# ScalarE and VectorE instruction order in a mixture-of-experts stage: scheduler's order or source order

## Chip, cores and metric

One core of a Trainium2 chip runs one program. The metric is device time in microseconds. Three runs of the kernel before gave 1894.52, 1895.95 and 1896.77; their median is 1895.95 us.

## What is computed

A hybrid layer, a retention layer and a Fourier layer, each with its feed-forward part, run over 256 tokens of width 1024 in float32. The change is in the last feed-forward part, a mixture of eight experts of which each token uses two:

```python
def swiglu(t, w_gate, w_up, w_down):
    return (jax.nn.silu(t @ w_gate) * (t @ w_up)) @ w_down

def moe_swiglu(h, w_router, w_gate, w_up, w_down):
    ...
    logits = (t @ w_router).astype(jnp.float32)
    top_val, top_idx = lax.top_k(logits, TOP_K)
    top_w = jax.nn.softmax(top_val, axis=-1)
    gates = jnp.sum(jax.nn.one_hot(top_idx, N_EXPERTS, dtype=jnp.float32) * top_w[..., None], axis=1)
    ...
    for e in range(N_EXPERTS):
        out = out + gates[:, e:e + 1] * swiglu(t, w_gate[e], w_up[e], w_down[e])
```

`w_gate` and `w_up` of an expert are 1024 x 3584, `w_down` is 3584 x 1024.

## The kernel before

**Weights.** All weights come as 1 MB units of 128 x 2048 float32, in the order in which TensorE uses them. SyncE issues one load a unit (line 113) into one of 13 buffers: six of `rawp`, four and two of the pools that `more_room` opens, and one in the space of `xT`. A unit is used as two *halves* of 128 x 1024. A half is split in two operands before TensorE takes it: ScalarE copies it to the short float type (line 139, tile `ringh` or `extrah`), and VectorE subtracts the copy from the original to get the rest (line 140, `ringl` or `extral`). There are six places for split halves: four in `ring`, two in `extra`, used in turn. A place is free when TensorE has done with the half in it; a raw buffer is free when VectorE has split its second half, and the next load waits for that.

**Keeping ahead.** `half` hands TensorE the oldest split half and first splits one more, so that in the source five halves stand split ahead of the one in use.

**One expert.** An expert is 84 halves in seven *strips*. In `experts`, `gate_strip` takes four halves (matmuls of lines 1154 to 1156) and ScalarE turns the sum into `sg` with Silu (line 1189). `up_strip` takes four more, and VectorE makes `h` of that sum and `sg` (line 1196). `turn` transposes `h` on TensorE (line 1206 or 1208); ScalarE and VectorE split the result into `hx` (lines 1212 and 1213). `down` takes four halves against `hx`. The `turn` of one strip lies in the middle of the next strip's gate, and its `down` behind the next strip's `up`; from the third strip on the cycle is: two gate halves, turn, two gate halves, four up halves, four down halves. At the expert's end `result` splits the two sums (lines 1245 and 1246), and `combine` adds them to `acc` during the next expert (lines 1265 to 1268).

**Packed experts.** In `up_strip`, `turn` and `down` a branch on TensorE (line 1162) takes one of two programs by the expert's number of tokens: with at most 64 (*packed*) a half costs four matmuls, otherwise six. Gate halves always cost six. In the trace, turns of line 1206 are packed ones: experts 0, 2, 3 and 4. Experts 1, 5, 6 and 7 are not.

**Hooks.** `nexth` counts halves and calls hooks at some of them: `gather` of the next expert's tokens (lines 1105 to 1124, at halves 77 to 83), `combine` (at 4 and 8) and, in expert 0, `weights_of_tokens` (at 4): about twenty small VectorE instructions, one Exp on ScalarE and one small matmul.

**What sets the order.** TensorE and SyncE run in source order in the whole kernel (`manual_schedule`). ScalarE and VectorE have no such rule in the experts: a scheduler places their instructions when the program is built. Each engine then executes its list from front to back, so that an instruction that waits holds those behind it.

Of the kernel before, what the change touches and what calls it, by code (L numbers as in the profile page):

```python
# [63 lines left out]
def kernel(  # L64
# [64 lines left out]
    def split(scales=None, between=None):  # L129


        if not raw or (half_[1] == H_F2 and scales is None):
            return
        wh, wl = place(half_[1])
        half_[1] += 1
        r = raw[0][0][:, half_[0] * HU:(half_[0] + 1) * HU]
        if scales is None:
            for o in (slice(0, HQ), slice(HQ, HU)) if half_[1] == 1 else (slice(0, HU),):
                nc.scalar.activation(out=wh[:, o], in_=r[:, o], func=AF.Copy)  # L139
                nc.vector.tensor_tensor(out=wl[:, o], in0=r[:, o], in1=wh[:, o].bitcast(F32), op=ALU.subtract)  # L140
                if between is not None and o.start == 0:
                    between()
        else:
            for t in range(2):
                o = slice(t * 512, t * 512 + 512)
                nc.scalar.activation(out=wh[:, o], in_=r[:, o], func=AF.Copy, scale=scales[:, t:t + 1])
                nc.vector.scalar_tensor_tensor(out=wl[:, o], in0=r[:, o], scalar=scales[:, t:t + 1],
                                               in1=wh[:, o].bitcast(F32), op0=ALU.mult, op1=ALU.subtract)
        wq.append((wh, wl))
        if half_[0]:  # L150
            fetch(raw.pop(0)[1])
        half_[0] ^= 1
# [39 lines left out]
    def bank(tag="mm", shape=(P, 2, S)):  # L192
        return psp.tile(list(shape), F32, tag=tag, name=tag, bufs={"mm": 4, "sd": 2, "dn": 2}[tag])
# [10 lines left out]
    def unitT(xh, xl):  # L204

        ps = bank()
        for cb in range(2):
            u = half()
            for k in range(KD):
                mm3T(ps[:, cb], u, k, xh[:, k], xl[:, k], k == 0, k == KD - 1)  # L210
        return ps

    def unit_late(xh, xl, late=2):

        ps = [bank("mm", (P, S)) for _ in range(2)]
        us = []
        for cb in range(2):
            us.append(half(ahead=not cb))
            for k in range(KD - late):
                mm3T(ps[cb], us[cb], k, xh[:, k], xl[:, k], k == 0, False)  # L220
        for cb in range(2):
            for k in range(KD - late, KD):
                mm3T(ps[cb], us[cb], k, xh[:, k], xl[:, k], False, k == KD - 1)
        split()
        return ps
# [159 lines left out]
    with pa:  # L385
# [264 lines left out]
        for i in range(8):  # L650
            ps = unitT(xh, xl)
            c, h = divmod(i, 2)
# [28 lines left out]
        for c in range(4, KD, 2):  # L681
            gg = []
            for _ in range(2):
                g = B.tile([P, 4, S], F32, tag="gate2", name="gate2")
                for h in range(2):
                    ps = unitT(xh, xl)
# [63 lines left out]
    with ExitStack() as pr:  # L750
# [120 lines left out]
        for c in range(KD):  # L871
            ps = bank("mm", (P, S))
# [23 lines left out]
    with ExitStack() as pn:  # L896
# [65 lines left out]
        def to_tok(src, c, tag):  # L962

            ps = bank(tag, (P, 2, S))
            for t in range(2):
                for b in range(2):
                    nc.tensor.transpose(ps[:, t, b * P:(b + 1) * P], src[c + b][:, t * P:(t + 1) * P], ident)
            return ps, slice(c * P, c * P + S)
# [18 lines left out]
        for cc in range(4):  # L987
            ps = unit_late(zh, zl) if cc == 0 else unitT(zh, zl)
# [34 lines left out]
        for c in range(0, KD, 2):  # L1023
            ps, o = to_tok(xT_, c, "mm")
            nc.scalar.activation(out=acc[:, :, o], in_=ps, func=AF.Copy)

        ps = bank("sd", (P, 3, E))
# [19 lines left out]
    def weights_of_tokens():  # L1047

        sel = [Q.tile([P, 2, E], F32, name=f"sel{i}") for i in range(2)]
        w12 = [Q.tile([P, 2], F32, name=f"w{i}") for i in range(2)]  # L1050
        tmp = Q.tile([P, 2, E], F32, name="tmp8")
        for i in range(2):
            nc.vector.tensor_scalar(out=sel[i], in0=cnt, scalar1=float(i), scalar2=None, op0=ALU.is_equal)
            nc.vector.tensor_tensor(out=tmp, in0=sel[i], in1=L, op=ALU.mult)
            nc.vector.tensor_reduce(out=w12[i], in_=tmp, axis=AX.X, op=ALU.add)
        nc.vector.tensor_tensor(out=w12[1], in0=w12[1], in1=w12[0], op=ALU.subtract)
        nc.vector.tensor_tensor(out=w12[1], in0=w12[1], in1=rcol, op=ALU.mult)
        nc.scalar.activation(out=w12[1], in_=w12[1], func=AF.Exp)
        nc.vector.tensor_scalar(out=w12[0], in0=w12[1], scalar1=1.0, scalar2=None, op0=ALU.add)
        nc.vector.reciprocal(out=w12[0], in_=w12[0])  # L1060
        nc.vector.tensor_tensor(out=w12[1], in0=w12[1], in1=w12[0], op=ALU.mult)
        for i in range(2):
            nc.vector.tensor_tensor(out=sel[i], in0=sel[i], in1=w12[i].unsqueeze(2).to_broadcast([P, 2, E]), op=ALU.mult)
        nc.vector.tensor_tensor(out=gts, in0=sel[0], in1=sel[1], op=ALU.add)
        ovf = Q.tile([P, 2], F32, name="ovf")
        nc.vector.tensor_scalar(out=tmp, in0=pos, scalar1=float(P), scalar2=None, op0=ALU.is_gt)
        nc.vector.tensor_reduce(out=ovf, in_=tmp, axis=AX.X, op=ALU.add)
        ps = bank("sd", (P, 2))
        mm(ps, ones, ovf, start=True, stop=True)
        nc.vector.tensor_copy(out=ovi, in_=ps)  # L1070
# [8 lines left out]
    with ExitStack() as pe:  # L1079
# [48 lines left out]
        def experts(ex, rs, half_fn, hooks=None, n_of=None):  # L1128
# [10 lines left out]
            def nexth(**kw):  # L1139
                if hooks and n[0] in hooks:  # L1140
                    hooks[n[0]]()
                n[0] += 1
                return half_fn(**kw)

            def hi_lo(x, items, packed):

                for out_, k, wh, wl, first, last in items:
                    xk = x[:, k].rearrange("p a b -> p (a b)")
                    if packed:
                        e = xk[:, HS:HS + P]  # L1150
                        mm(out_, e, wh, start=first, stop=False)
                    else:
                        e = xk[:, 0:P]
                        mm(out_, e, wh, start=first, stop=False)  # L1154
                        mm(out_, xk[:, P:2 * P], wh, start=False, stop=False)  # L1155
                    mm(out_, e, wl, start=False, stop=last)  # L1156
# [10 lines left out]
            def strip_items(ps, h, w):  # L1167
                return [(ps, 2 * h + kk, w[0][:, kk * 512:(kk + 1) * 512], w[1][:, kk * 512:(kk + 1) * 512],
                         h + kk == 0, h == 3 and kk == 1) for kk in range(2)]

            def strip(mid=None):
                ps = bank("mm", (P, 512))
                for h in range(4):
                    if h == 2 and mid is not None:
                        mid()
                    hi_lo(ex, strip_items(ps, h, nexth()), False)
                return ps

            def pair(f):
# [80 lines left out]
        def combine(res, sot, gcol, hfs=range(2)):  # L1260
            for hf in hfs:
                yh, yl = res[hf]
                for t in range(2):
                    ps = bank("sd", (P, 512))
                    mm(ps, sot[:, t], yh, start=True, stop=False)
                    mm(ps, sot[:, t], yl, start=False, stop=True)
                    o = slice(hf * 512, hf * 512 + 512)
                    nc.vector.scalar_tensor_tensor(out=acc[:, t, o], in0=ps, scalar=gcol(t), in1=acc[:, t, o],
                                                   op0=ALU.mult, op1=ALU.add)

        def gath(e):
            return gather(lambda t: pos[:, t, e:e + 1], lambda t: posu[:, t, e:e + 1])
# [4 lines left out]
        nxt = gath(0)  # L1277
# [3 lines left out]
        while len(wq) < WB + WX - 1:  # L1281
            split()
        last = None
        for e in range(E):
            ex, sot, rs, _ = nxt
            if last:
                hooks = {4: lambda a=last: combine(*a, (0,)), 8: lambda a=last: combine(*a, (1,))}
            else:
                hooks = {1: nxt[3][4], 4: weights_of_tokens}
            if e + 1 < E:  # L1290
                nxt = gath(e + 1)
                hooks.update(zip((77, 79, 80, 82, 83), nxt[3]))
            last = (experts(ex, rs, half, hooks, lambda: n_of(e)), sot, lambda t, e=e: gts[:, t, e:e + 1])
            if e == 0:
                n_over = [nc.values_load(ovi[0:1, t:t + 1], min_val=0, max_val=2 * S) for t in range(2)]
        v4 = Q.tile([P, 2, 2], F32, name="v4")
        v = Q.tile([P, 2], F32, name="fv")
        r = Q.tile([P, 2], F32, name="fr")
# [21 lines left out]
        with tc.tile_pool(name="O", bufs=1) as O:  # L1320
# [5 lines left out]
            with tc.If(n_over[0] + n_over[1] > 0):  # L1326

                nc.vector.tensor_copy(out=ecur, in_=io8)
                with tc.For_i(0, E, 1) as ev:
# [21 lines left out]
                    oex, osot, ors, steps = gather(lambda t: epos[:, t:t + 1], lambda t: epos[:, t:t + 1])  # L1351
# [179 lines left out]
```

## Time and profile before

| | |
|---|---|
| median of three runs | 1895.95 us |
| the profiled execution, its own time | 1900.18 us |
| its span in the profile | 1898.4 us |
| TensorE, matmuls | 1827.2 us, 96% of the span |
| VectorE | 1474.8 us, 78% |
| ScalarE | 1198.2 us, 63% |
| first and last Silu of the experts begin at | 912.4 and 1864.1 us |

Time lines count from the start of the span. The experts fill the second half of it. A busy share is an average over stages that have different limits: for a change in the experts it must be read there, expert by expert and strip by strip.

### The profile page before, as it was taken

What the parts mean: (1) busy time and instruction counts of PE and PEld (TensorE: products, weight loads), DVE (VectorE), ACT (ScalarE), POOL (GpSimd) and SP (SyncE); (2) the same over time, 40 slices, a digit from 0 to 9 for tenths busy, and PEclk for the clock granted to TensorE, in tenths of its full rate; (3) what the DMA queues carried; (4) which work ended last, traced back from release to release, by engine and by line L of the source; (5) the groups of instructions that cost most, each with busy time, mean ns of one, the idle gap of its engine ahead of it and who ended that gap; (6) DMA issues with size and microseconds to landing.
All of it is one profiled execution on the core that took longest, in us unless ns stands there. A gap on an engine that the chain in (4) does not pass through costs nothing. (4 is left out here: it accounts for less than half of the span.)

```text
span 1898.4 us, 28758 instructions
## 1 busy us (share of the span) xinstructions
PE 1827.2 (96%) x10890; PEld 1576.7 (83%) x10890; DVE 1474.8 (78%) x1855; ACT 1198.2 (63%) x1484; POOL 158.6 (8%) x154
## 2 busy tenths in 40 slices
PE   8999999999999999999999999999999999999996
PEld 7999999998888999998777886666676778788785
DVE  5666676657776666556899889899899988988887
ACT  5765454445444444445887777777777877767774
POOL 2302122211100122101000000000000000000000
PEclk9999999999999999999999999999999999999998
DMA  7344555555344654454799998999999999899880
GB/s 308 136 154 174 182 178 183 195 178 195 139 160 155 239 218 178 180 199 158 295 421 370 353 364 329 373 359 362 378 350 369 362 352 368 336 354 363 322 334 35
DMA packets 71156, 505.77 MB, mean 266 GB/s; under 512 B 7888, under 2 KB 8016, under 8 KB 10320
## 3 DMA queue, kind: packets, MB, share of 16 engines
q1 hardware_dynamic: 70992, 503.53, 70.5%
q8 instruction: 110, 1.80, 0.4%
q14 instruction: 54, 0.44, 0.1%
HBM read 502.45 MB, written 1.05 MB: 265 GB/s over the span
## 5 line engine op out<-in xcount | busy, mean ns | idle before, releaser
L140 DVE TENSOR_TENSOR ringl<-raw,ringh 128x1024 fp32r<-128x1024 f32 (+1 forms) x694 | 828.7, 1228 | 191.9 <-ACT ringh L139 186.6
L139 ACT ACTIVATE ringh<-raw 128x1024 fp32r<-128x1024 f32 (+1 forms) x694 | 703.4, 1050 | 309.0 <-PE mm L201 192.1
L200 PE MATMUL mm<-xh,ringh 128*128 128x256 f32 x1248 | 357.4, 286 | 6.4 <-ACT xh L354 6.4
L202 PE MATMUL mm<-xh,ringl 128*128 128x256 f32 x1248 | 354.7, 284 | 1.5 <-DVE ringl L140 1.5
L201 PE MATMUL mm<-xl,ringh 128*128 128x256 f32 x1248 | 355.1, 285 | 1.0 <-DVE xl L355 0.7
L140 DVE TENSOR_TENSOR extral<-raw,extrah 128x1024 fp32r<-128x1024 f32 x206 | 244.4, 1221 | 66.3 <-ACT extrah L139 66.3
L200 PEld LDWEIGHTS mm<-xh,ringh 128*128 128x128 f32 x1248 | 238.0, 191 | 7.8 <-ACT xh L354 6.4
L201 PEld LDWEIGHTS mm<-xl,ringh 128*128 128x128 f32 x1248 | 237.8, 191 | 2.3 <-DVE xl L355 2.1
L202 PEld LDWEIGHTS mm<-xh,ringl 128*128 128x128 f32 x1248 | 237.7, 190 | 1.9 <-DVE ringl L140 1.9
L139 ACT ACTIVATE extrah<-raw 128x1024 fp32r<-128x1024 f32 x206 | 207.6, 1050 | 10.2 <-PE mm L1155 8.2
L1156 PE MATMUL mm<-ringl,ex 128*128 128x512 f32 x480 | 191.0, 398 | 0.0
L1156 PE MATMUL mm<-extral,ex 128*128 128x512 f32 x416 | 168.0, 404 | 17.3 <-DVE extral L140 17.0
L1156 PE MATMUL dn<-ringl,hx 128*128 128x512 f32 x416 | 170.5, 410 | 0.0
L1154 PE MATMUL mm<-ringh,ex 128*128 128x512 f32 x352 | 144.4, 410 | 0.0
L1155 PE MATMUL mm<-ringh,ex 128*128 128x512 f32 x352 | 139.8, 397 | 0.2 <-DVE ex L1115 0.2
L1154 PE MATMUL mm<-extrah,ex 128*128 128x512 f32 x320 | 125.5, 392 | 0.0
L1155 PE MATMUL mm<-extrah,ex 128*128 128x512 f32 x320 | 125.4, 392 | 0.0
L1156 PEld LDWEIGHTS mm<-extral,ex 128*128 128x128 f32 x416 | 78.0, 187 | 53.4 <-DVE extral L140 38.2
L1156 PEld LDWEIGHTS mm<-ringl,ex 128*128 128x128 f32 x480 | 90.6, 189 | 24.1 <-DVE ringl L140 2.3
L1156 PEld LDWEIGHTS dn<-ringl,hx 128*128 128x128 f32 x416 | 78.2, 188 | 38.6 <-DVE ringl L140 23.1
L202 PE MATMUL mm<-hh,ringl 128*128 128x256 f32 x352 | 99.6, 283 | 0.0
L200 PE MATMUL mm<-hh,ringh 128*128 128x256 f32 x352 | 99.6, 283 | 0.0
(420 smaller groups left out, 3158.8 us busy)
## 6 DMA issues: line engine op xcount, KB each, us to landing
raw<-in_ws_dram SPq DMA_DIRECT2D x448, 1024.0 KB, 6.7
xT<-in_ws_dram SPq DMA_DIRECT2D x25, 1024.0 KB, 7.5
raw<-in_ws_dram SPq DMA_DIRECT2D x3, 512.0 KB, 7.8
xT<-in_xT_dram SPq DMA_DIRECT2D x4, 256.0 KB, 4.7
xT<-in_xT_dram SPq DMA_DIRECT2D x1, 1024.0 KB, 8.2
out_dram<-acc SPq DMA_DIRECT2D x4, 256.0 KB, 2.1
cstA<-in_cst_dram SPq DMA_DIRECT2D x1, 576.0 KB, 9.5
raw<-in_ws_dram SPq DMA_DIRECT2D x2, 256.0 KB, 4.2
```

Source lines behind the costliest of these rows:

```text
L139: nc.scalar.activation(out=wh[:, o], in_=r[:, o], func=AF.Copy)
L140: nc.vector.tensor_tensor(out=wl[:, o], in0=r[:, o], in1=wh[:, o].bitcast(F32), op=ALU.subtract)
L200: mm(ps, wh[:, c], xh, start=start, stop=False)
L201: mm(ps, wh[:, c], xl, start=False, stop=False)
L202: mm(ps, wl[:, c], xh, start=False, stop=stop)
L1154: mm(out_, e, wh, start=first, stop=False)
L1155: mm(out_, xk[:, P:2 * P], wh, start=False, stop=False)
L1156: mm(out_, e, wl, start=False, stop=last)
```

## The change

ScalarE and VectorE get source order from the start of the experts' loop to its end (`manual_schedule`, closed behind the loop). For that, three things in the source move: `strip` now asks for its third half before it calls the turn, `weights_of_tokens` becomes a generator whose four steps run at halves 4, 5, 6 and 7, and the load of the two overflow counts (`values_load` of `ovi`, on every engine) now stands where the source has it.

```diff
@@ -1055,7 +1055,9 @@
             nc.vector.tensor_reduce(out=w12[i], in_=tmp, axis=AX.X, op=ALU.add)
         nc.vector.tensor_tensor(out=w12[1], in0=w12[1], in1=w12[0], op=ALU.subtract)
         nc.vector.tensor_tensor(out=w12[1], in0=w12[1], in1=rcol, op=ALU.mult)
+        yield
         nc.scalar.activation(out=w12[1], in_=w12[1], func=AF.Exp)
+        yield
         nc.vector.tensor_scalar(out=w12[0], in0=w12[1], scalar1=1.0, scalar2=None, op0=ALU.add)
...
@@ -1065,6 +1067,7 @@
         nc.vector.tensor_reduce(out=ovf, in_=tmp, axis=AX.X, op=ALU.add)
+        yield
         ps = bank("sd", (P, 2))
...
@@ -1171,9 +1174,10 @@
                 for h in range(4):
+                    w = nexth()
                     if h == 2 and mid is not None:
                         mid()
-                    hi_lo(ex, strip_items(ps, h, nexth()), False)
+                    hi_lo(ex, strip_items(ps, h, w), False)
                 return ps
...
@@ -1281,18 +1285,22 @@
         last = None
+        order = ExitStack()
+        order.enter_context(tc.manual_schedule(engines={mybir.EngineType.Activation, mybir.EngineType.DVE}))
         for e in range(E):
...
             else:
-                hooks = {1: nxt[3][4], 4: weights_of_tokens}
+                steps = weights_of_tokens()
+                hooks = {1: nxt[3][4], **{h: lambda: next(steps, None) for h in (4, 5, 6, 7)}}
...
             if e == 0:
                 n_over = [nc.values_load(ovi[0:1, t:t + 1], min_val=0, max_val=2 * S) for t in range(2)]
+        order.close()
```

TensorE's and SyncE's lists keep their order, but for the small matmul of `ovf`, which comes three halves later. On ScalarE the moved pieces are these. Expert 3, one strip of the steady cycle, before (L139 is a split, `hx` line 1212, `sg` line 1189):

```order
L139 ACTIVATE extrah<-raw 128x1024
L139 ACTIVATE ringh<-xT 128x1024 x2
L1162 UNCONDITIONAL_BRANCH
L139 ACTIVATE ringh<-raw 128x1024 x2
L1212 ACTIVATE hx<-sd 128x4x128
L1189 ACTIVATE sg<-mm,rsl 128x512
L139 ACTIVATE extrah<-raw 128x1024
```

The same place now:

```order
L139 ACTIVATE ringh<-raw 128x1024 x2
L139 ACTIVATE extrah<-raw 128x1024
L1165 UNCONDITIONAL_BRANCH
L139 ACTIVATE extrah<-raw 128x1024
L1216 ACTIVATE hx<-sd 128x4x128
L139 ACTIVATE ringh<-raw 128x1024
L1165 UNCONDITIONAL_BRANCH
L1193 ACTIVATE sg<-mm,rsl 128x512
```

`hx` and `sg` stood side by side, in front of the two `extra` splits; now `hx` stands behind these two and `sg` behind one split more. Counted in the lists, the splits that stand ahead of `sg`, beyond the halves that it needs, were 2 in most strips of experts 2 to 7 (4 in the second strip) and are now 5 everywhere; for `hx` they were 4 and are 6 (5 at an expert's last turn). In expert 0 they were 6 and 6 before, and are 5 and 6.

On VectorE the same strip was:

```order
L140 TENSOR_TENSOR ringl<-raw,ringh 128x1024 x2
L1196 SCALAR_TENSOR_TENSOR h<-mm,rsl,sg 128x512
L1162 UNCONDITIONAL_BRANCH
L140 TENSOR_TENSOR extral<-raw,extrah 128x1024 x2
L140 TENSOR_TENSOR ringl<-xT,ringh 128x1024 x2
L1162 UNCONDITIONAL_BRANCH
L140 TENSOR_TENSOR ringl<-raw,ringh 128x1024 x2
L1213 TENSOR_TENSOR hx<-sd,hx 128x4x128
```

and is now:

```order
L140 TENSOR_TENSOR extral<-raw,extrah 128x1024
L1200 SCALAR_TENSOR_TENSOR h<-mm,rsl,sg 128x512
L140 TENSOR_TENSOR extral<-raw,extrah 128x1024
L140 TENSOR_TENSOR ringl<-xT,ringh 128x1024 x2
L1165 UNCONDITIONAL_BRANCH
L140 TENSOR_TENSOR ringl<-raw,ringh 128x1024 x2
L1165 UNCONDITIONAL_BRANCH
L140 TENSOR_TENSOR extral<-raw,extrah 128x1024 x2
L1217 TENSOR_TENSOR hx<-sd,hx 128x4x128
```

`h` comes one split later and `hx` two. The two loads of `ovi` on VectorE, which stood behind the last `L307` of the kernel, now stand at the end of expert 0:

```order
L1250 TENSOR_TENSOR y<-dn,y 128x512 x2
L140 TENSOR_TENSOR ringl<-raw,ringh 128x1024
L1302 TENSOR_LOAD ovi x2
L1097 TENSOR_SCALAR so<-cst,pos 128x64
```

They left the end of the program for a place with eight hundred microseconds of work behind it.

## Rows read from the trace of the kernel before

**Rows 1.** Busy time of each engine over the whole span, from the page.
```profile
PE 1827.2 (96%) x10890; PEld 1576.7 (83%) x10890; DVE 1474.8 (78%) x1855; ACT 1198.2 (63%) x1484; POOL 158.6 (8%) x154
```
**Rows 2.** Busy time by stretch: stretch, length, engines, clock, DMA share, GB/s; experts 0, 2, 3, 4, 5.
```profile
912.41:1020.97 108.56, 103.01 (x463) 81.30 (x462) 102.58 (x102) 92.59 (x103) 0.00 (x0) 0.98 0.96 388
...
1148.10:1268.86 120.76, 111.55 (x479) 81.34 (x478) 110.80 (x112) 91.74 (x104) 0.00 (x0) 1.00 0.94 359
1268.86:1389.59 120.73, 111.49 (x479) 81.40 (x478) 111.10 (x113) 91.77 (x105) 0.00 (x0) 1.00 0.96 365
1389.59:1511.30 121.71, 112.54 (x479) 82.85 (x478) 111.16 (x113) 91.75 (x105) 0.00 (x0) 0.99 0.96 362
1511.30:1637.77 126.47, 125.74 (x563) 101.51 (x562) 111.46 (x113) 92.30 (x105) 0.00 (x0) 1.00 0.95 357
```
**Rows 3.** The same for one strip, Silu to Silu, of experts 0, 3 and 5.
```profile
968.26:983.12 14.86, 14.74 (x65) 10.99 (x64) 14.86 (x15) 12.94 (x16) 0.00 (x0) 1.00 1.02 422
1298.56:1315.26 16.70, 15.56 (x65) 10.86 (x64) 14.97 (x14) 12.66 (x14) 0.00 (x0) 1.00 0.92 368
1542.63:1559.77 17.14, 17.14 (x77) 13.87 (x76) 14.98 (x14) 12.66 (x15) 0.00 (x0) 1.00 0.90 343
```
**Rows 4.** Timeline, one strip of expert 3: start, length, engine, instruction, wait before it.
```profile
1312.46 0.60 ACT L1212 ACTIVATE hx<-sd 128x512 fp32r<-128x512 f32 x1 [1.84 <-PE sd L1206]
1314.52 0.69 DVE L1213 TENSOR_TENSOR hx<-sd,hx 128x512 fp32r<-128x512 f32 x1
1315.26 0.69 ACT L1189 ACTIVATE sg<-mm,rsl 128x512 f32<-128x512 f32 x1 [2.20 <-PE mm L1156]
1315.85 2.00 ACT L139 ACTIVATE extrah<-raw 128x1024 fp32r<-128x1024 f32 x2
1316.93 2.36 DVE L140 TENSOR_TENSOR extral<-raw,extrah 128x1024 fp32r<-128x1024 f32 x2 [1.73 <-ACT extrah L139]
1318.21 0.50 PE L1156 MATMUL mm<-extral,ex 128*128 128x512 f32 x1 [0.77 <-DVE extral L140]
1320.16 0.40 PE L1151 MATMUL dn<-ringh,hx 128*128 128x512 f32 x1
```
**Rows 5.** Waits in experts 2 to 4: who waited for whom, us in all, times, longest.
```profile
ACT sg L1189 <- PE mm L1156: 43.5, 21, 3.0
...
DVE extral L140 <- ACT extrah L139: 26.2, 15, 1.8
...
ACT xs L1107 <- DVE h L1196: 3.2, 3, 1.1
```
**Rows 6.** Timeline of VectorE in expert 0, four splits in a row.
```profile
977.33 4.63 DVE L140 TENSOR_TENSOR ringl<-raw,ringh 128x1024 fp32r<-128x1024 f32 x4
```
**Rows 7.** DMA traffic from 950 to 1000 us, in expert 0.
```profile
DMA packets 2885, 21.04 MB, mean 421 GB/s; under 512 B 320, under 2 KB 320, under 8 KB 320
```
**Rows 8.** Timeline: the issue of the last weight loads (SPq) and ScalarE's last split.
```profile
1836.20 6.01 SPq L113 DMA_DIRECT2D raw<-in_ws_dram  x4
...
1874.68 1.05 ACT L139 ACTIVATE ringh<-raw 128x1024 fp32r<-128x1024 f32 x1
```
**Rows 9.** Waits from 1511 to 1864 us, experts 5 to 7.
```profile
PEld sd L1208 <- DVE h L1196: 3.0, 3, 1.0
```
**Rows 10.** The loads of `ovi` on VectorE's queue, and the timeline behind them.
```profile
L1295 DVEq TENSOR_LOAD <-ovi x2: 320/435/550, 1890.7 to 1891.3; - x2
...
1892.59 0.75 DVE L1363 SCALAR_TENSOR_TENSOR acc<-acc,fr,xT 128x512 f32<-128x512 f32 x1 [1.85 <-DVEq L1326]
```
**Rows 11.** Timeline, start of expert 0: `rcol` ready, ScalarE's table load, the first turn.
```profile
905.10 0.15 DVE L307 SCALAR_TENSOR_TENSOR rcol<-rs,rsy 128x2 f32<-128x2 f32 x1
905.30 1.28 ACT L1058 ACT_TABLE_LOAD   x1
...
919.57 0.77 PE L1206 MATMUL sd<-cst,h 128*128 128x128 f32 x2 [2.71 <-DVE h L1196]
```

## Prediction

> **What bounds the kernel now.** I read the busy shares first. TensorE is busy for 96% of the span [rows 1], which suggests that nothing off TensorE can matter. That is an average over stages, so the next view is busy time by stretch, expert by expert [rows 2]. The reader should compare VectorE (third busy figure) with each stretch's length. In expert 0 VectorE is busy for 102.58 of 108.56 us. The packed experts 2, 3 and 4 do the same splits with the same program on TensorE, yet take 120.76, 120.73 and 121.71 us with VectorE at 110.80, 111.10 and 111.16: it idles 9.96, 9.63 and 10.55 us, together 30.1. Expert 5, unpacked, has TensorE busy for 125.74 of 126.47 us.
>
> The same view of one strip [rows 3] shows three limits. In expert 0 the strip takes 14.86 us, and VectorE is busy for all of it. In expert 3 it takes 16.70 with VectorE at 14.97: 1.73 us are lost. In expert 5 it takes 17.14, all of it TensorE's. TensorE's busy time in a packed strip is not a fixed amount of work: 65 matmuls count 15.56 us in expert 3 and 14.74 in expert 0, since a matmul that is held up is shown longer.
>
> The timeline of expert 3 [rows 4] tells why the 1.73 us are lost. ScalarE has done `hx` at 1313.06 and then stands 2.20 us at `sg`, which needs the last gate matmul. Only at 1315.85 does it go on with splits. VectorE has nothing to subtract and waits 1.73 us for `extrah`, TensorE then 0.77 us for `extral`. Over experts 2 to 4 the wait at `sg` sums to 43.5 us in 21 strips, and the listed waits of VectorE on `extrah` to 26.2 [rows 5]. The order lists show the reason: two splits stand ahead of `sg` beyond the halves that it needs, where expert 0 had six. Expert 0 is thus a trial, inside this very run, of an order with a long lead.
>
> **The change, part by part.** All sums are against the profiled execution of 1900.18 us (its span is 1898.4). It is 4.2 us longer than the median of the three runs, 1895.95; I apply the difference that I work out to the median.
>
> *Packed experts 2 to 4.* `sg` now has five splits ahead of it everywhere. TensorE uses a half each 14.86/12 = 1.24 us in such a strip, so five last 6.2 us. What has to fit in is `sg` (0.69), ScalarE's next split (1.05 [rows 8]) and VectorE's rest of it (half of 2.36, so 1.18 [rows 4]): 2.9 us. VectorE should then never run dry, and the strip falls to its own work. That work is twelve splits at 4.63/4 = 1.16 us at most [rows 6], `hx` at 0.69 [rows 4] and `h`: about 14.9, as the 14.86 and the 14.97 already say. Of the 30.1 us of idleness I leave 1.0 an expert: ScalarE's `xs` waits for VectorE's `h` in the gather, 3.2 us in three experts [rows 5], and `h` now comes later still. That gives **−27.1 us**. The bounds are −30.1 (no residue) and −24.1 (twice the residue).
>
> *Unpacked experts 1, 5, 6 and 7.* Their strips are TensorE's 17.14 us, and VectorE with 14.98 us of work [rows 3] has slack, so nothing is to be gained inside them. But TensorE waits for `h` at the first turn of an expert, 1.0 us each in experts 5 to 7 [rows 9], where the scheduler put splits ahead of it. In source order `h` stands behind the splits of fixed lead only: **−3**, bounds 0 and −4 (expert 1 too).
>
> *`hx` two splits later.* Two splits of VectorE cost at most 2.36 us [rows 4]. `hx` ends at 1315.21, and the first matmul that reads it begins at 1320.16 [rows 4], 4.95 us later. The cover is the four up halves, which TensorE does first. Cost: nothing. If the cover were gone, each strip would pay up to 2.36 us.
>
> *The loads of `ovi`.* At present VectorE executes two TENSOR_LOADs (0.55 and 0.32 us) at the very end, and the last addition waits 1.85 us behind its queue [rows 10]. At expert 0's end they stand in VectorE-bound work, which then pays for them once; but there VectorE also had idle time waiting for others (108.56 against 102.58 [rows 2]). Tail: **−0.9**. Expert 0's end, where VectorE no longer waits for what the scheduler put ahead: **−1**, bounds 0 and −1.7 (one stall as in expert 3's strip).
>
> *`weights_of_tokens` in four steps.* About twenty small VectorE instructions, 0.15 us for one such [rows 11], move from ahead of expert 0 into its first strips, which are VectorE's: up to 3 us. Against that, TensorE's first turn waits 2.71 us for `h` at present [rows 11], which hides part. ScalarE's table load for Exp (1.28 [rows 11]) and the one back to Silu also move behind `sg` of the first strip. I take **+1.3**, nearer the middle, as half of the work has that wait to lie in; bounds 0 and +3.
>
> *Transfers.* A faster expert needs its weights faster. Expert 3 moved 365 GB/s for 120.73 us, 44.1 MB; in 111.8 us that is 394 GB/s. Expert 0 held 388 over its whole length [rows 2], 422 in a strip [rows 3], and 421 for 50 us [rows 7]. I cost it at nothing, covered by the loads that are under way ahead of use. The Trainium skill, "DMA: Bandwidth & Descriptors" (Where 436 GB/s comes from), speaks against this: it says that for transfers from HBM the limit of about 358 GB/s for a core binds; by it, an estimate, an expert could not take less than 44.1/0.358 = 123 us, and the packed experts would gain nothing. The 421 GB/s of the trace contradict that for this core, and the measurement decides.
>
> *End of the stream.* The last weight loads are issued by 1842.2, and ScalarE's last split is at 1874.68 [rows 8]: no transfer is on the final chain, so that gains in the middle reach the end.
>
> Sum: −27.1 − 3 − 0.9 − 1 + 1.3 = **−30.7 us**; 1900.18 becomes 1869.5, and the median 1865.2, which I round to **1865.5**. All bounds on the good side give −36.7 (1859), on the bad side −24.1 + 3 − 0 = −21.1 (1875).
>
> **The rivals.** *Half the gain.* `h` also moved one split back, and it waits for `sg`; if VectorE stands there for the sum and for ScalarE in turn, part of the stall survives. Halfway between 0 and 1.73 us is 0.87 a strip, 18 us in 21 strips: about 1883. For it: the lead falls on two engines that wait for each other. Against it: expert 0, with nearly this order and VectorE 14.86 of 14.86 [rows 3]. Chance 0.08.
>
> *Transfers become the bound.* The loads keep to the 359 to 365 GB/s of experts 2 to 4, where the DMA share is already 0.94 to 0.96 [rows 2]. The packed experts stay at 121 us, and what is left is −3.6: about 1892, no measurable change. Against it: 421 GB/s for 50 us [rows 7], and a share of 1.02 in expert 0's strip [rows 3]: 0.95 is no ceiling. Chance 0.04. It is the page's rule as a mechanism of this kernel.
>
> *Slower.* ScalarE in source order stands at `sg` until the last gate matmul, behind one split more; VectorE and TensorE live on the lead. If the lead that is really there is under the 2.9 us of the chain (two unpacked halves of 17.14/12 = 1.43 us), TensorE runs dry in the 28 strips of unpacked experts too, where before it never did. The price is the 0.77 us that TensorE waits in expert 3 [rows 4]: 28 × 0.77 = 21.6, with nothing gained in packed ones and the small terms at −0.6: about 1917. For it: six places for split halves, one in use, leave nothing over five. Against it: 2.9 is far below 5 × 1.43 = 7.1. Chance 0.03.
>
> *The order is not what the change says*, since something else fixes it: 1896. The order lists speak against it; chance 0.01.
>
> **How the numbers follow.** The forecast has 0.84, half the gain 0.08, transfers 0.04, slower 0.03, no effect 0.01. About 0.2%, 3.8 us, is what a measurement can tell from no change. Faster: 0.84 + 0.08 = 0.92; same: 0.04 + 0.01 = 0.05; slower: 0.03. The range is the sum's bounds, 1859 to 1875, with one or two microseconds for the scatter of runs (1894.5 to 1896.8): 1858 to 1877. That holds nearly all of the first case and leaves out about 2 in 10.
>
> **What would show it.** Right: packed strips of 14.9 us in experts 2 to 4, experts of about 112, VectorE busy for 99% of them, no wait of 2.2 us at `sg` that passes on to VectorE and TensorE, DMA near 394 GB/s, unpacked strips still 17.1 without the wait for `h`, and a shorter wait ahead of the last addition. Wrong: packed strips of 16 us or more, with VectorE waiting for `extrah` still (half the gain), ScalarE or VectorE waiting for a DMA at some 360 GB/s (transfers), or TensorE waiting for splits in unpacked strips (slower).

## The result and the profile after

The changed kernel takes **1869.43 us** (1866.96 to 1871.62, four runs) against 1896.03 of the kernel before, measured beside it: 0.986 of the time, 95% interval 0.9843 to 0.9877. That is 26.6 us less. Forecast were 30.5 less, 1865.5, with a range of 1858 to 1877.

A second measurement of the same changed kernel, beside the last experiments, gave 1870.77 and 0.9851 (0.9837 to 0.9866).

The page of the changed kernel shows the same work in a shorter span:

```profile
PE 1813.6 (97%) x10890; PEld 1584.7 (85%) x10890; DVE 1483.7 (79%) x1855; ACT 1218.6 (65%) x1484; POOL 158.6 (8%) x154
```

As in [rows 1], this average says nothing about the experts. Busy time by stretch does (stretch, length, PE, PEld, DVE, ACT, POOL, clock, DMA share, GB/s). These are experts 0, 2, 3, 4 and 5 of the changed kernel, from Silu to Silu, and answer to [rows 2]:

```profile
909.12:1025.22 116.10, 108.21 (x473) 84.32 (x472) 108.22 (x124) 96.31 (x107) 0.00 (x0) 0.96 0.92 371
1150.86:1261.16 110.30, 105.94 (x479) 82.77 (x478) 109.74 (x113) 93.48 (x104) 0.00 (x0) 1.00 0.99 400
1261.16:1373.81 112.65, 107.54 (x479) 84.20 (x478) 110.59 (x113) 93.44 (x105) 0.00 (x0) 0.98 0.98 392
1373.81:1486.50 112.69, 107.57 (x479) 84.17 (x478) 110.64 (x113) 93.47 (x105) 0.00 (x0) 0.98 0.97 393
1486.50:1612.10 125.60, 125.31 (x563) 101.89 (x562) 114.08 (x113) 96.64 (x104) 0.00 (x0) 1.00 0.93 352
```

Experts 2 to 4 took 363.20 us and now take 335.64, and VectorE is busy in nearly all of it. Expert 5 is 0.9 us shorter. Expert 0 is *longer*, by 7.5 us. One steady strip of experts 3 and 5, as in [rows 3]:

```profile
1305.21:1320.09 14.88, 14.78 (x65) 10.97 (x65) 14.88 (x15) 12.97 (x14) 0.00 (x0) 1.00 1.02 424
1517.56:1534.70 17.14, 17.14 (x77) 13.93 (x76) 15.41 (x15) 13.37 (x15) 0.00 (x0) 1.00 0.96 372
```

The packed strip is VectorE's, 14.88 of 14.88 us; the unpacked one is TensorE's still. The timeline of the packed strip shows what became of the stall of [rows 4] (start, length, engine, instruction, wait before it):

```profile
1317.30 0.60 ACT L1216 ACTIVATE hx<-sd 128x512 fp32r<-128x512 f32 x1
1318.47 1.06 ACT L139 ACTIVATE ringh<-raw 128x1024 fp32r<-128x1024 f32 x1 [0.57 <-DMA raw<-in_ws_dram]
1319.57 2.35 DVE L140 TENSOR_TENSOR extral<-raw,extrah 128x1024 fp32r<-128x1024 f32 x2
1320.10 0.69 ACT L1193 ACTIVATE sg<-mm,rsl 128x512 f32<-128x512 f32 x1 [0.57 <-PE mm L1159]
1320.69 2.00 ACT L139 ACTIVATE ringh<-raw 128x1024 fp32r<-128x1024 f32 x2
1321.84 0.68 DVE L1217 TENSOR_TENSOR hx<-sd,hx 128x512 fp32r<-128x512 f32 x1
```

ScalarE still waits for the last gate matmul at `sg`, but for 0.57 us in place of 2.20, and VectorE does not wait at all. The waits of experts 2 to 4 in the changed kernel (who, for whom, us in all, times, longest) answer to [rows 5]:

```profile
ACT sg L1193 <- PE mm L1159: 11.2, 22, 0.6
...
ACT xs L1110 <- DVE h L1200: 10.4, 3, 3.5
...
PE sd L1210 <- DVE acc L1272: 6.0, 3, 2.3
...
ACT ringh L139 <- DMA raw<-in_ws_dram: 2.8, 5, 0.6
```

43.5 us at `sg` became 11.2. The wait at `xs` grew from 3.2 to 10.4. Two waits appeared that were not there before: TensorE's turn waits for VectorE's `acc`, the addition of `combine`, in the first strip of each of the three experts, and ScalarE waits for the DMA.

**Where the 26.6 us come from.** In the two profiled executions I count from the first matmul of expert 0 (902.26 before, 898.91 after) to the end of the span, 996.1 and 970.9 us: 25.3 less. The time ahead of that matmul differs from execution to execution (896.57 to 902.26 in the profiles of this study), while the experts of the changed kernel agree within 0.6 us in two executions, so that differences in the experts are read from the trace.

| term | forecast | trace |
|---|---|---|
| experts 2 to 4 | −27.1 | −27.6 |
| from the first expert matmul to expert 1's first Silu (118.71, now 126.31) | +1.3 − 1 | +7.6 |
| unpacked experts 1, 5 and 6 (127.13, 126.47, 126.49; now 125.63, 125.61, 125.07), and 7 with the tail (134.14, now 132.61) | −3 − 0.9 | −5.3 |
| sum | −30.7 | −25.3 |

The term that is furthest off is the start. Of its 7.6 us, 4.8 lie in expert 0's first strip (13.42 us before, now 18.22) and 2.3 in its last (22.96, now 25.27). The timeline of the changed kernel shows the first of the two, on TensorE:

```profile
902.64 0.66 PE L1125 MATMUL sd<-rcol,so 128*128 128x1 f32 x4 [1.41 <-DVE rcol L307]
...
915.80 0.56 PE L1072 MATMUL sd<-ovf,ones 128*128 128x2 f32 x2 [4.90 <-DVE ovf L1069]
916.23 0.77 PE L1154 MATMUL mm<-ringh,ex 128*128 128x512 f32 x1
916.80 0.63 PE L1159 MATMUL mm<-ringl,ex 128*128 128x512 f32 x1
917.22 0.63 PE L1154 MATMUL mm<-ringh,ex 128*128 128x512 f32 x1
917.65 0.63 PE L1159 MATMUL mm<-ringl,ex 128*128 128x512 f32 x1
```

The last of the four steps of `weights_of_tokens` issues the small matmul of `ovf` on TensorE. It waits 4.90 us for VectorE, whose chain up to `ovf` runs through ScalarE's Exp with its table load and stands behind splits. Behind it matmuls follow each other at 0.43 us, where the same trace has 0.23 at full clock. Busy time by stretch shows the granted clock (third column from the end) behind each of the two waits, and where it is back:

```profile
903.16:906.30 3.14, 3.14 (x9) 2.46 (x9) 1.62 (x3) 0.62 (x1) 0.00 (x0) 0.50 0.75 297
906.61:910.43 3.82, 3.82 (x18) 3.15 (x17) 2.97 (x7) 2.50 (x4) 0.00 (x0) 1.00 0.30 86
915.80:919.78 3.98, 3.98 (x10) 3.21 (x11) 1.82 (x3) 1.18 (x2) 0.00 (x0) 0.50 0.61 202
920.18:922.70 2.52, 2.52 (x12) 2.06 (x11) 2.12 (x4) 1.61 (x3) 0.00 (x0) 1.00 0.34 143
```

It is 0.50 of full speed, 1.2 GHz, in both. In the kernel before there was one such stretch, behind the wait at the first turn [rows 11]:

```profile
919.57:923.00 3.43, 3.43 (x12) 3.14 (x13) 2.81 (x3) 0.60 (x1) 0.00 (x0) 0.51 0.61 225
```

### The profile page after: what moved, and what is told of

Its sections match the earlier page's. It is cut to its first block, busy times and chain, and to the rows that moved or that the text cites. A ratio compares the mean times of both kernels' runs of the same rounds, so it can differ in the third digit from the quotient of the medians.

```text
span 1869.8 us, 28869 instructions
## 1 busy us (share of the span) xinstructions
PE 1813.6 (97%) x10890; PEld 1584.7 (85%) x10890; DVE 1483.7 (79%) x1855; ACT 1218.6 (65%) x1484; POOL 158.6 (8%) x154
## 5 line engine op out<-in xcount | busy, mean ns | idle before, releaser
L139 ACT ACTIVATE ringh<-raw 128x1024 fp32r<-128x1024 f32 (+1 forms) x694 | 710.4, 1052 | 352.3 <-PE mm L201 192.4
L140 DVE TENSOR_TENSOR extral<-raw,extrah 128x1024 fp32r<-128x1024 f32 x206 | 249.0, 1219 | 11.4 <-ACT extrah L139 11.2
L139 ACT ACTIVATE extrah<-raw 128x1024 fp32r<-128x1024 f32 x206 | 212.4, 1054 | 48.4 <-PE mm L1158 31.3
L201 PE MATMUL mm<-hl,ringh 128*128 128x256 f32 x352 | 99.6, 283 | 0.0
```

The costliest lines, as they stand in the source:

```text
L201: mm(ps, wh[:, c], xl, start=False, stop=False)
```

## The experiments

**Theory A:** ScalarE's lead at `sg`, the splits that stand ahead of it beyond the halves that it needs, decides the packed experts. **Theory B:** the places of `h` and `hx` on VectorE, or other choices of the scheduler, do. The first two runs give source order to one engine alone.

### ScalarE alone, VectorE alone

```diff
-order.enter_context(tc.manual_schedule(engines={mybir.EngineType.Activation, mybir.EngineType.DVE}))
+order.enter_context(tc.manual_schedule(engines={mybir.EngineType.Activation}))
```

(the second run has `mybir.EngineType.DVE` in its place)

> Only ScalarE follows the source in the experts; VectorE's order is the scheduler's (h with four splits ahead, as before; hx with six). Theory A, ScalarE's lead at sg decides: packed strips of experts 2 to 4 at 14.9 us, time 1866 to 1873. Theory B, the places of h and hx on VectorE decide: h is back at its old place, so at least half of the packed gain of 27.5 us goes, time above 1880.

> Only VectorE follows the source in the experts; ScalarE's order is the scheduler's, and sg has two splits ahead in most strips, as before. Theory A: packed strips stay at 16.7 us, time 1890 to 1896 (what is left is TensorE's wait for h in unpacked experts, 3 to 5 us). Theory B: packed strips at 14.9, time about 1869.

ScalarE alone: **1866.22 us**, ratio 0.9829 (0.9803 to 0.9854). VectorE alone: **1934.82**, ratio 1.0181 (1.0156 to 1.0207), slower than before. Busy time by stretch, expert 3 and a steady strip of it, with ScalarE alone:

```profile
1254.22:1364.70 110.48, 106.29 (x479) 82.74 (x478) 110.41 (x113) 94.00 (x105) 0.00 (x0) 1.00 1.00 399
1296.98:1311.86 14.88, 14.51 (x65) 11.13 (x64) 14.88 (x15) 13.01 (x15) 0.00 (x0) 1.00 1.01 420
```

and with VectorE alone, with an unpacked strip as the last row:

```profile
1281.53:1408.47 126.94, 114.36 (x479) 83.93 (x478) 111.17 (x113) 92.19 (x104) 0.00 (x0) 0.97 0.92 348
1329.76:1346.84 17.08, 15.66 (x65) 10.80 (x64) 14.97 (x14) 12.66 (x15) 0.00 (x0) 1.00 0.96 348
1584.86:1602.07 17.21, 17.21 (x77) 13.80 (x76) 14.97 (x14) 12.67 (x14) 0.00 (x0) 1.00 0.95 364
```

Theory A holds: ScalarE's order carries the whole gain, with `h` at its old place. Theory B falls: `hx` on VectorE is at its new place in both runs and brings nothing in the second. VectorE's source order is rather a cost in the trace: with ScalarE alone experts 2 to 4 take 331.37 us where the changed kernel takes 335.64, and the start, from the first expert matmul to expert 1's first Silu, 117.50 (with the clock at 1.00) where it takes 126.31. In time the two can't be told apart (0.9829 and 0.986, with intervals that overlap). But VectorE alone was expected at 1890 to 1896 and took some 40 us more, 38 more than the kernel before (1897.16, measured beside it). Its timeline in the steady strip of expert 3:

```profile
1329.76 0.69 ACT L1193 ACTIVATE sg<-mm,rsl 128x512 f32<-128x512 f32 x1 [2.20 <-PE mm L1159]
1330.34 1.99 ACT L139 ACTIVATE extrah<-raw 128x1024 fp32r<-128x1024 f32 x2
1331.42 2.36 DVE L140 TENSOR_TENSOR extral<-raw,extrah 128x1024 fp32r<-128x1024 f32 x2 [2.11 <-ACT extrah L139]
1333.70 0.69 DVE L1217 TENSOR_TENSOR hx<-sd,hx 128x512 fp32r<-128x512 f32 x1
```

ScalarE's wait at `sg` is the old one. VectorE now has `hx` *behind* the two `extra` splits, while ScalarE has it ahead of `sg`: what VectorE used to do while ScalarE stood (0.69 us at 1314.52 in [rows 4]) is locked behind the splits that are late. Its wait grows from 1.73 to 2.11. The larger part lies at the start, which this run shares with the changed kernel (126.87 us against 118.71), and at the experts' ends: in experts 5 and 6 VectorE waits up to 5.4 us for one split, as the waits from 1520 to 1800 us list:

```profile
DVE extral L140 <- ACT extrah L139: 32.8, 12, 5.4
```

### Fewer splits ahead of `sg`

Both engines keep source order, but some splits of the gate halves come behind `sg` (three, for a lead of two; two, with `h < 2` in the first line, for a lead of three):

```diff
                 for h in range(4):
-                    w = nexth()
+                    w = nexth(ahead=h < 1) if half_fn is half else nexth()
...
                 nc.scalar.activation(out=sg[s], in_=ps, func=AF.Silu, scale=rs)
+                if half_fn is half:
+                    for _ in range(3):
+                        split()
```

> The changed kernel, but the splits that belong to the second, third and fourth gate half come behind sg, so that two splits stand ahead of it and hx (four ahead) stands beside it, as before the change; both engines in source order. Theory A: the chain of 2.9 us outlasts two halves of 1.24 us, VectorE waits some 1.7 us a strip, packed strips at 16.7, time 1869 + 21 x 1.8 to 1.9 = about 1897 or somewhat more (expert 0 has the short lead too now). Theory B, that the scheduler's other choices cost the time: about 1870.

> As the one with two, but only the splits of the third and fourth gate half come behind sg: three ahead. Theory A, a threshold: three halves last 3.7 us against the 2.9 of the chain, so packed strips stay near 14.9 and the time near 1869 to 1873. Rival, a loss in proportion to the lead that is missing (two of three steps back to before): about 1887.

A lead of two: **1945.35 us**, ratio 1.0245 (1.0218 to 1.0271). A lead of three: **1908.15**, ratio 1.0045 (1.0026 to 1.0064). With five it was 0.986. A steady packed strip with two, and one with three:

```profile
1344.83:1361.31 16.48, 15.59 (x65) 10.79 (x64) 14.98 (x15) 12.65 (x14) 0.00 (x0) 1.00 0.99 386
```

```profile
1329.08:1344.42 15.34, 15.21 (x65) 10.88 (x64) 14.97 (x15) 12.66 (x14) 0.00 (x0) 1.00 1.01 420
```

The lead is the cause: 16.48, 15.34 and 14.88 us for two, three and five. My sum for three was wrong, though: 1908 lies above the 1869 to 1873 of theory A and above the rival's 1887. I compared the chain of 2.9 us with the halves that *TensorE* still had (3 × 1.24 = 3.7). The timeline of the run with three shows who runs dry:

```profile
1329.08 0.69 ACT L1193 ACTIVATE sg<-mm,rsl 128x512 f32<-128x512 f32 x1 [2.20 <-PE mm L1159]
1329.66 1.05 ACT L139 ACTIVATE extrah<-raw 128x1024 fp32r<-128x1024 f32 x1
1329.69 0.69 DVE L1220 TENSOR_TENSOR hx<-sd,hx 128x512 fp32r<-128x512 f32 x1
...
1330.74 1.23 DVE L140 TENSOR_TENSOR extral<-raw,extrah 128x1024 fp32r<-128x1024 f32 x1 [0.36 <-ACT extrah L139]
```

It is VectorE. It follows ScalarE by a few splits, so that its reserve is what ScalarE has copied and it has not yet subtracted. ScalarE's absence is the wait at `sg` (2.20) as well as `sg` and the next copy, 3.9 us; VectorE's reserve lasts 0.36 less, in every strip.

The totals are above before's, although the steady strips of experts 2 to 4 are not. With two, counted from the first expert matmul, the run is 46.8 us longer than the kernel before (1042.92 and 996.14). 22.3 of these lie in expert 0, where before's scheduler had a lead of six (its steady strip is 16.48 here, 14.86 there); 8.1 of the 22.3 are its first strip, in which TensorE waits 8.5 us for `ovf`, so they are not the lead's alone. 12.9 lie in experts 2 to 4, in their last strips (1.4 to 2.7 each), their first (1.8 each) and their second, which had a lead of four before (15.03 and now 16.49 in expert 3). The rest is in unpacked experts, 2 to 4 each. Their steady strips keep 17.14. So it is true, as the rival "slower" has it, that a fixed lead which is too short makes this order slower than the kernel before; against that kernel the point lies between three and five splits, and the change stands on the right side of it. The rival's own mechanism, TensorE running dry in unpacked strips, does not appear even with a lead of two.

### The place of the turn

```diff
                 for h in range(4):
-                    w = nexth()
                     if h == 2 and mid is not None:
                         mid()
-                    hi_lo(ex, strip_items(ps, h, w), False)
+                    hi_lo(ex, strip_items(ps, h, nexth()), False)
```

> The changed kernel without the move in strip: the turn is called ahead of the third gate half's split, so that hx has five splits ahead on both engines, not six. If the place of hx matters little (the cover of 4.95 us in the prediction): packed strips 14.9, time 1868 to 1872. If hx with five ahead is what made packed strips 15.35 us in the run with three splits ahead of sg (which had it too): 15.3 here, time about 1880 or more.

**1870.14 us**, ratio 0.9853 (0.9834 to 0.9872). Steady packed strips are 14.88 us, as in the changed kernel. The move in `strip` changes nothing that can be measured, and the 15.34 of the run with three ahead of `sg` belong to `sg`.

### The start

```diff
-hooks = {1: nxt[3][4], **{h: lambda: next(steps, None) for h in (4, 5, 6, 7)}}
+hooks = {1: nxt[3][4], **{h: lambda: next(steps, None) for h in (4, 5, 6, 30)}}
```

> The changed kernel with the last step of weights_of_tokens (the small matmul of ovf and the copy to ovi) at half 30 in place of 7. Theory C: in the changed kernel TensorE stands 4.9 us at that matmul for VectorE's chain, and its clock falls for some 4 us behind it, which expert 0 pays; then the matmul finds ovf ready, expert 0 falls from 116.1 to about 111, and the time by 3 to 5 us, to 1864 to 1867. Rival, the small VectorE instructions themselves cost it, as the prediction had it: no change, 1868 to 1871.

**1869.34 us**, ratio 0.9848 (0.9831 to 0.9866). In time this run can't be told from the changed kernel, and the 1864 to 1867 of theory C did not come. In the trace the wait at `ovf` is gone, and the clock stays at 1.00 from 900 to 930 us (0.83 in the changed kernel). From the first expert matmul to expert 1's first Silu, of this run and of the changed kernel:

```profile
898.06:1018.93 120.87, 113.10 (x505) 88.22 (x504) 114.43 (x138) 99.79 (x112) 0.00 (x0) 0.99 0.94 374
```

```profile
898.91:1025.22 126.31, 117.01 (x505) 91.17 (x504) 114.89 (x137) 100.08 (x111) 0.00 (x0) 0.94 0.90 358
```

5.4 us less, but not all of it is the edit's. Split at expert 0's first Silu, the stretch of this run is:

```profile
898.06:906.64 8.58, 7.05 (x34) 5.56 (x33) 6.69 (x15) 3.78 (x5) 0.00 (x0) 1.00 0.66 244
906.64:1018.93 112.29, 106.05 (x473) 82.66 (x472) 107.74 (x124) 96.01 (x108) 0.00 (x0) 0.98 0.96 384
```

The changed kernel takes 10.21 us to that Silu, with the fallen clock behind the wait at `rcol`, which stands ahead of everything that the edit moves. That makes 1.6 of the 5.4 us; expert 0 itself is 3.8 shorter, 112.29 for 116.10. The profiled execution is also the fastest of four: 1865.42 us at a mean granted clock of 0.993, the others 1869.03 to 1869.87 at 0.989 to 0.990. So the trace shows that the wait is gone, and the time does not show a gain.

To see one in the time too, the next run also takes the other three steps out of expert 0; they stand ahead of the part in source order:

```diff
+steps = weights_of_tokens()
+for _ in range(3):
+    next(steps)
 order = ExitStack()
...
-hooks = {1: nxt[3][4], **{h: lambda: next(steps, None) for h in (4, 5, 6, 7)}}
+hooks = {1: nxt[3][4], 30: lambda: next(steps, None)}
```

> The changed kernel, but the first three steps of weights_of_tokens stand ahead of the part in source order, where the scheduler places them, and only the matmul of ovf is left in expert 0, at half 30. Theory C: all that the start lost against before lies in these instructions and the wait for them; from the first expert matmul to expert 1's first Silu 117 to 119 us (before 118.7, changed kernel 126.3), time 6 to 9 below the changed kernel of the same call. Rival, the start is lost to the shorter lead of sg in expert 0 (five for six): 124 or more, time within 2 of the changed kernel.

**1864.54 us**, ratio 0.9826 (0.9813 to 0.9839), 6.2 us below the changed kernel measured beside it (1870.77). The stretch, in the kernel before and in this run:

```profile
902.26:1020.97 118.71, 112.28 (x505) 88.71 (x504) 111.91 (x137) 100.21 (x111) 0.00 (x0) 0.98 0.91 366
```

```profile
897.99:1018.76 120.77, 114.00 (x505) 89.67 (x504) 113.75 (x135) 99.85 (x111) 0.00 (x0) 0.97 0.93 374
```

That is 5.5 shorter than in the changed kernel, though the clock falls behind the wait at `rcol` here as it does there, and 2 longer than before. So the four steps in expert 0 make 5.5 of the 7.6 us, and here the time shows it. By an estimate from these rows some 4 of the 5.5 are the wait at `ovf` with the clock behind it, and the rest the other instructions; no run parts them cleanly. Theory C holds in the main; its 117 to 119 us were too few. The last 2 us lie in expert 0's last strip, 25.14 us in this run and 22.96 before. With `h` one split earlier (the run of that name below) this strip takes 23.09.

### The loads of `ovi`

```diff
-            if e == 0:
-                n_over = [nc.values_load(ovi[0:1, t:t + 1], min_val=0, max_val=2 * S) for t in range(2)]
         order.close()
...
         out_rms()
+        n_over = [nc.values_load(ovi[0:1, t:t + 1], min_val=0, max_val=2 * S) for t in range(2)]
```

> The changed kernel, but the two loads of ovi stand at the end of the program again, ahead of the last branch. Theory D: the loads cover the time in which VectorE's queue comes by the code behind its branch, so the gap ahead of the last addition goes back from 3.03 to about 1.85 us, and the time falls by about 1. Rival, the loads are a cost of their own (0.9 us) and the branch keeps its 2.8 us: the gap grows to about 3.9.

**1873.87 us**, ratio 0.9868 (0.9847 to 0.9888). The timeline shows the first of the last additions and the wait ahead of it, in the changed kernel, in this run, and in the run with the turn first:

```profile
1863.98 2.74 DVE L1371 SCALAR_TENSOR_TENSOR acc<-acc,fr,xT 128x512 f32<-128x512 f32 x4 [3.03 <-DVEq L1334]
```

```profile
1867.00 2.74 DVE L1370 SCALAR_TENSOR_TENSOR acc<-acc,fr,xT 128x512 f32<-128x512 f32 x4 [4.12 <-DVEq L1333]
```

```profile
1860.09 0.75 DVE L1370 SCALAR_TENSOR_TENSOR acc<-acc,fr,xT 128x512 f32<-128x512 f32 x1 [0.76 <-DVEq L1333]
1862.34 2.08 DVE L1370 SCALAR_TENSOR_TENSOR acc<-acc,fr,xT 128x512 f32<-128x512 f32 x3 [1.49 <-issue]
```

Theory D falls, and the rival holds. The loads cost 1.1 us of their own (4.12 less 3.03), about the 0.9 of the prediction. The branch ahead of the additions costs some 3 us in both, and in the other profiles too: the wait is 3.03 to 3.31 us where the loads stand at expert 0's end, but for the run with the turn first, and 4.10 to 4.21 in the two runs of ScalarE alone, where they stand at the end. In the kernel before, 1.85 less the loads leaves about 0.8 [rows 10]. In the run with the turn first it is 0.76 and a second gap of 1.49 behind the first addition. No edit here touches the code behind that branch; only its place in the program differs. The Trainium skill, "Runtime: NRT & Kernel Launch" (Instruction fetch mechanics), says that a taken branch whose target lies outside what has been fetched has to wait for a DMA of the code. The 0.8 and 3.0 us fit that, and no run here shows it by itself.

### `h` one split earlier, and the gather later

```diff
-def pair(f):
+def pair(f, then=None):
...
     either(lambda packed: f(w, packed))
+    if then is not None:
+        then()
     if half_fn is half:
         split()
```

`up_strip` passes the lines that make `h` as `then` with its second pair.

> The changed kernel with h ahead of the last split of its up strip on VectorE: four splits ahead of it, as in the scheduler's order, where the changed kernel has five. Theory E: the 3.5 us that ScalarE waits for h at xs, at the ends of experts 2 and 3, shorten by one split, 1.2 us, and with it the ends of packed experts: 1 us less in each of experts 3 and 4, strips unchanged, time 1866 to 1869. Rival, h with four ahead makes VectorE wait for TensorE's up halves: packed strips above 15, time above 1871.

**1868.42 us**, ratio 0.9841 (0.9817 to 0.9865): not to be told from the changed kernel by time. By the trace theory E holds in kind: the longest wait at `xs` falls from 3.5 to 2.1 us, and experts 2, 3 and 4 take 109.66, 111.93 and 112.01 us, 0.7 less each where 1 was expected. The end of expert 0 gains most, 2.2 us (its last strip 23.09 for 25.27).

```diff
-hooks.update(zip((77, 79, 80, 82, 83), nxt[3]))
+g = nxt[3]
+hooks.update({78: g[0], 80: g[1], 81: g[2], 83: lambda g=g: (g[3](), g[4]())})
```

> ScalarE alone in source order, with the gather of the next expert at halves 78, 80, 81 and 83 in place of 77 to 83. If ScalarE's wait for h at xs still costs: it goes (2.1 us each in the run of ScalarE alone), packed experts 110.4 become 109.5, time 1 to 3 us lower than 1866. Rival, VectorE is the bound there and the wait is covered: no change in experts 2 to 4, and TensorE may wait for tokens at the start of each expert, time 1866 to 1872.

**1865.97 us**, ratio 0.9832 (0.9818 to 0.9846), the same as ScalarE alone. The wait for `h` at `xs` is gone, and experts 2 to 4 take 332.95 us against 331.37: no gain, as the rival had it.

### Put together

This run has the start with only the matmul of `ovf` left at half 30, `h` ahead of the last split, and the later gather too, which its expectation leaves out.

> The same start, and h ahead of the last split of its up strip. Both gains are apart in place, so they should add: experts 2 to 4 some 0.7 us shorter each than with the start alone, time 2 to 3 us below it. Rival, VectorE-bound strips take back what h gives: the same as with the start alone.

> The changed kernel itself, to have it beside the others in one call: 1867 to 1872.

**1860.73 us** (1858.77 to 1864.07), ratio 0.9812 (0.9797 to 0.9828); the changed kernel beside it took 1870.77, 0.9851 (0.9837 to 0.9866). This beats both kernels: 10 us less than the changed one and 37.3 less than before (1898.05, measured beside it). It is 3.8 below the start alone. Experts 2 to 4 take 331.78 us for 335.49, 3.7 less, of which `h` alone had given 2.0; what the gather adds beside it was not run apart. Busy time of experts 0, 2 and 3:

```profile
911.06:1017.55 106.49, 102.10 (x468) 80.74 (x467) 104.82 (x107) 93.28 (x104) 0.00 (x0) 1.00 0.97 397
1142.86:1252.70 109.84, 105.05 (x479) 83.18 (x478) 109.84 (x113) 93.66 (x104) 0.00 (x0) 1.00 0.99 400
1252.70:1364.61 111.91, 106.63 (x479) 84.48 (x478) 110.89 (x113) 93.80 (x104) 0.00 (x0) 0.98 0.98 396
```

Expert 2 is VectorE's from end to end, 109.84 of 109.84 us.

## Why the prediction was right, and where it was not

- **Packed experts: right in cause; in size two misses cancel.** −27.6 for −27.1, strips of 14.88 for 14.9. The idle time of VectorE that is left is 4.7 us and not 3.0, but its busy time in the three experts also fell by 2.1 us (333.1 to 331.0), which the sum took as fixed. Expert 0 of the kernel before was a fair trial of the long lead. The runs with two and three splits ahead show the cause; the run with ScalarE alone shows that it lies on that engine.
- **The lead sum: right by luck of its margin.** "2.9 us against 6.2" measured TensorE's reserve. VectorE's is shorter, and ScalarE's wait at `sg` belongs to the chain. With three splits the same sum promised no loss, and 0.36 us a strip were lost.
- **The residue: right in kind, low, and in part at another place.** I left 1.0 us an expert for the gather. VectorE is idle for 0.6, 2.1 and 2.0 us in experts 2 to 4. About 0.6 of each lies at the expert's end, where `xs` waits up to 3.5 us for `h`, and goes with `h` one split earlier. The other 1.5 us of experts 3 and 4 lie in their first two strips, where TensorE's turn waits up to 2.3 us for `acc` of `combine` and ScalarE 3.5 at `hx` for the turn; the prediction has no such term, and no run takes this wait away by itself.
- **`weights_of_tokens` in four steps, +1.3: the step that failed.** I counted the small instructions on VectorE and the table loads, and not that the last step is a matmul on TensorE, which executes in order and stands still for it: 4.90 us, with half the clock behind. The number of instructions was no news for expert 0: in the kernel before most of them ran behind the first expert matmul (902.26) already, from 904.33 to 910.90, and `ovf` was ready at 905.40 for its matmul at 910.00. What was lost is that lead. With the −1 for expert 0's end, which did not come either (there ScalarE's wait for `h` at `xs` grew from 0.6 to 3.5 us), the start was +7.6 for +0.3. That is more than the 4 us by which the forecast missed.
- **Unpacked experts: right in kind, low by half.** −3 was the wait for `h`, which is gone from the waits of experts 5 to 7 [rows 9]. It lay in their first strips, which are 0.3, 0.8 and 0.8 us shorter, 1.9 in place of 3. Yet experts 1, 5 and 6 alone gave 3.8, and expert 7 2.7 if the tail's 1.2 is taken out: 6.5. The last strips of experts 1, 5 and 6 are 0.5 us shorter each and expert 1's first strip 1.7; why, I did not test.
- **The tail, −0.9: right as a term, and outdone.** The loads cost 1.1; the branch took some 2 us more than before, so that the wait ahead of the last addition grew, 3.03 for 1.85, where the prediction named a shorter one as a sign of being right.
- **Transfers: no bound.** 392 to 400 GB/s against the forecast 394. The 358 GB/s that the prediction cites from the Trainium skill, "DMA: Bandwidth & Descriptors" (Where 436 GB/s comes from), do not bind this core.
- **The range:** the sum of the bad bounds leaves out the −0.9 of the tail; with it, it is −22.0 and 1874 in place of 1875.

## What to carry over

On engines that execute in order, count for every instruction that waits how much work stands ahead of it that others live on, and measure it in the reserve of the engine that runs dry first: here VectorE behind ScalarE, not TensorE. A scheduler that puts two waiting instructions side by side spends that reserve at once; source order with a fixed lead keeps it. When pieces are moved by hand, follow each instruction they issue to the engine that it lands on: a step of two small matmuls (0.56 us) made TensorE stand for 4.90, because everything of TensorE stood behind it.

## What was not expected of the hardware

- VectorE in source order with ScalarE left to the scheduler is worse than the kernel before by 38 us, and worse than both engines in source order. Some 8 of the 38 lie at the start, which the changed kernel loses too. That the two lists disagree on the order of `hx` and the splits shows in a steady packed strip as a wait of 2.11 us for 1.73; for the experts' ends I did not take it apart.
- TensorE's clock fell to 0.50 for some 3 to 4 us behind waits of 1.41 and 4.90 us in the changed kernel. In the profile of the run with the late matmul it waited 1.3 us at the same `rcol` and kept 1.00 throughout, while after the same 1.3 us the clock fell in the changed kernel's second profile and in those of the runs with the loads at the end, the turn first and `h` earlier. What tells them apart is open.
- The branch ahead of the last additions cost about 0.8 us in the kernel before and about 3 in others with the same code behind it.
- At 392 to 400 GB/s ScalarE begins to wait for a raw buffer's data, up to 0.6 us at a time and 2.8 us in experts 2 to 4, in steady packed strips still hidden behind VectorE.
